# Row transposes of the first four key chunks tied to later projections in a hand-planned attention list

## The chip, the cores and the metric

The kernel runs on one core of a Trainium2 chip. The metric is the device time of one execution in microseconds (us). The core has five engines with in-order queues of their own: TensorE (PE in the profile, with its weight loads as PEld), VectorE (DVE), ScalarE (ACT), GpSimd (POOL) and SyncE (SP), which here issues most of the transfers.

## The reference

One inference step of a two-layer decoder trunk, for a new sequence of 512 tokens (prompt) and for 8 sequences of 4 new tokens each with 256 past tokens in a paged key/value cache (sample). Layer 0 mixes tokens with a gated convolution, layer 1 with stick-breaking attention; each layer ends in a convolutional feed-forward network (FFN). All data are 32-bit floats; the model width is 1024, with 16 heads of 64.

```python
def stick_breaking_block(q, k, v, bias, q_start):
    z = jnp.einsum('bqhd,bkhd->bhqk', q, k) * (HEAD_DIM ** -0.5) + bias
    valid = k_pos < q_pos
    log_fail = jnp.where(valid, jax.nn.log_sigmoid(-z), 0.0)
    after = lax.cumsum(log_fail, axis=3, reverse=True) - log_fail
    weights = jnp.where(valid, jnp.exp(jax.nn.log_sigmoid(z) + after), 0.0)
    return jnp.einsum('bhqk,bkhd->bqhd', weights, v)

# layer 1
qkv = (h @ attn_w_qkv).reshape(b, t, 3, N_HEADS, HEAD_DIM)
q, k, v = qkv[:, :, 0], qkv[:, :, 1], qkv[:, :, 2]
att = stick_breaking_attention(q, concat(k_past, k), concat(v_past, v), bias, past_len)
x = x + att.reshape(b, t, -1) @ attn_w_o
new_k.append(k); new_v.append(v)      # the new K and V rows are outputs too
```

The last line is what the change is about: the new keys, token by token, are an output of the kernel.

## The kernel before, in words

All 544 tokens are worked on together, transposed: a chunk of 128 features lies on the 128 partitions and the tokens along the free dimension. A matrix product is made from 128x128 weight blocks that are split into a high and a low part (`whi` by ACT, line 401, `wlo` by DVE, line 404) and three matmuls for each block (lines 2150 to 2152 in the attention stage). Tokens are taken in two halves, the first with 256 columns and the second with 288.

The stages are layer 0's convolution, its FFN together with the queries and the first four key chunks of layer 1, the attention stage, layer 1's FFN and the final norm. In each stage the code does not issue instructions directly. It fills a list (`Plan`) with operations, each with an engine, an assumed cost and what it reads and writes; `Plan.run` then goes through the list with those assumed costs as a clock and so settles, before the kernel is compiled, in which order each engine gets its work. For an engine that comes free it takes an operation that is ready or soon will be, by the assumed time, with a bonus of 0.04 us for each microsecond of work that hangs on it (`EAGER`). Operations marked as fill are taken when nothing else is ready soon, or when their bonus outweighs the wait. The chip then runs each engine's queue strictly in that order, whatever the real times are.

The attention list is built by the calls at the end of the listing. For each of the 8 chunks of two heads it holds `keys(c, h)` and `values(c, h)` for the two token halves h, `page_logits` for the decode sequences' cached keys, and `pair(c)`, the prompt's attention for the two heads of a chunk:

- `project(slot, h)` (line 2159) adds four fill operations on PE, a quarter each, of six matmuls, into a bank `acc` (two of them). All projections follow one another in the order v0, v1, v2, k4, v3, k5, v4, k6, v5, k7, v6, v7, each with both halves.
- `to_rows` (line 2174) turns two 128x128 blocks into token rows with two PE transposes (line 2180) into the bank `one`, of which there is only one.
- `keys` (line 2185): for c of 4 and up it projects the chunk first. For c below `EARLY_K` = 4 the keys are already there from the stage before. Either way it calls `to_rows`, copies the rows to a buffer `kr` (DVE, line 2195; two buffers) and stores them to the output (SP, line 2196, 128 KB).
- `values` (line 2199): projects, copies to a buffer `vT` (ACT, line 2203; two buffers), calls `to_rows`, and copies the rows to `vtok` (DVE, line 2207), which the products `av` of `pair` read (line 2475).
- `page_logits`: pages of cached keys, gathered by POOL (line 2042) into three buffers, are transposed in halves of four PE transposes (line 2271) into a bank `t` (one of them) and copied from it by DVE or ACT in turn (line 2278). The second half of the very first page goes to a bank `dz` instead. The list allows 3.0 us before the first pages are there.

Banks and buffers with a name are handed out as a ring: the n-th user of the name waits for the user that held the same bank before, in the order in which the code asks for them. Rows of key chunks 0 and 1 are asked for ahead of the first values, rows of chunk 2 and 3 one and two rounds later. The decode sequences' weights use the bank `one` four times, ahead of the rows of k4.

Of the kernel before, what the change touches and what calls it, by code (L numbers as in the profile page):

```python
# [17 lines left out]
P = 128  # L18
# [27 lines left out]
EARLY_K = 4  # L46
# [204 lines left out]
def tile_trunk(  # L251
# [8 lines left out]
    nc = tc.nc  # L260
    dve, act, pool, pe = nc.vector, nc.scalar, nc.gpsimd, nc.tensor
# [210 lines left out]
    def uid(s):  # L472
        _n[0] += 1
        return f"{s}_{_n[0]}"
# [38 lines left out]
    def begin(n, ready, s0, st, xh, xl):  # L513

        pts = [bank("acc", uid("acc")) for _ in range(n)]
        for i, pt in enumerate(pts):
            gemm(pt, st, s0 + i, xh, xl, None, (0, ready))
        return pts
# [193 lines left out]
    for i in range(2):  # L712
        ch0 = (PE_CHUNKS[0] + i * len(PE_CHUNKS) // 2) * P
        for m in range(8):
            nj = min(4, CW - 4 * m)
            pool.dma_start(out=trow[i][m * n_g:(m + 1) * n_g, :nj * 32].rearrange("g (j h) -> g j h", j=nj),
                          in_=conv_w_dw[0, 4 * m:4 * m + nj, ch0:ch0 + n_g * 32].rearrange("j (g h) -> g j h", h=32))
# [4 lines left out]
    plan = Plan(E_CONV, 0.12, CONV_SHIFTS)  # L722
# [14 lines left out]
    def psum(tag):  # L737
        def make():
            if tag == "acc":
                taken.append(tag)  # L740
            return bank(tag, uid(tag))

        return plan.tile(tag, banks[tag], make)
# [27 lines left out]
    def prepare(slot, begin, place):  # L771

        low = []
        raw = slot // 2
        plan.op("act", 0.95, lambda: begin(low), r=[("raw", slot)], w=[*place, ("slot", slot), "prep"])
        plan.op("dve", 1.135, lambda: low[0](), r=[("raw", slot)], w=[("slot", slot), "low"])
        if slot % 2:
            plan.op(f"raw{raw}", 5.4 if raw else 8.6, lambda: None, w=[("raw", slot + 2 * RAW_BUFS + i) for i in (-1, 0)], r=[("slot", slot)])
# [50 lines left out]
    def conv_vector(c, lo, n):  # L829


        acc = buf(conv, "dwh", [P, 256], 1) if n == 256 else buf("ctmp", "dwa", [P, SEQ], 2)
        keys = ext(c) if n > 256 else ext(c, 1, 2, 3) if lo else ext(c, 0, 1)
        done = ext(c) if n > 256 else ext(c, 1, 2, 3) if lo else ext(c, 0)
        halves = [("y", c, h) for h in range(2) if lo <= 256 * h < lo + n]
        cost = n * 1.05e-3 + 0.126
        for k in range(CW):
            src = ext_p[:, c, lo + k:lo + k + n]
            if k == 0:
                plan.op("act", 0.28 + n * 0.85e-3, lambda src=src: act.activation(  # L840
                    acc()[:, :n], src, AF.Identity, scale=pcol(0, c), bias=pcol(R_BDW, c)), r=[*keys, "prm"], w=[acc])
            elif k < CW - 1:
                plan.op("dve", cost, lambda k=k, src=src: dve.scalar_tensor_tensor(
                    acc()[:, :n], src, pcol(k, c), acc()[:, :n], op0=ALU.mult, op1=ALU.add),
                    r=[*keys, "prm"], w=[acc])
            else:
                plan.op("dve", cost, lambda k=k, src=src: dve.scalar_tensor_tensor(
                    yc[:, c, lo:lo + n], src, pcol(k, c), acc()[:, :n], op0=ALU.mult, op1=ALU.add),
                    r=[acc, "prm"], w=halves + done)
# [55 lines left out]
    def add_sum(c, h):  # L905
        c0, n = STREAMS[h]
        if c == 0:
            return
        keys = [("y", i, k) for i in ((0, 1) if c == 1 else (c,)) for k in ((1, 2) if h else (0,))]

        def add():
            o = late["ysum"][:, c0:c0 + n]
            dve.tensor_tensor(o, yc[:, c, c0:c0 + n], yc[:, 0, c0:c0 + n] if c == 1 else o, op=ALU.add)

        plan.op("dve", 0.08 + n * 1.05e-3, add, r=keys, w=[("sum", h)])
# [191 lines left out]
    for c in range(0, NC, 2):  # L1107
# [9 lines left out]
        for cc in range(2):  # L1117
            plan.op("act", 0.33, lambda c=c, cc=cc, pt=pt: act.copy(
                ext_s[:, c + cc, :, 0:PAST], pt()[:, cc * 240:(cc + 1) * 240].rearrange("p (b t) -> p b t", b=NB)),
                r=[pt, "junk"], w=[("past", c + cc)])  # L1120
# [124 lines left out]
    for h, (c0, n) in enumerate(STREAMS):  # L1245
        if h:
            layer_norm(1)
        for g in (0, 4):
            for i in range(4):
                c = g + i  # L1250
# [5 lines left out]
        if not h:  # L1256
# [8 lines left out]
            r=[nrm.acc[0]], w=[ms])  # L1265
    plan.op("act", 0.34, lambda: act.activation(rs()[:, :n], ms()[:, :n], AF.Sqrt, bias=eps_t[:, 0:1], scale=1.0),
            r=[ms, "table"], w=[rs])
    plan.op("dve", 1.7, lambda: dve.reciprocal(rs()[:, :n], rs()[:, :n]), w=[rs])
    for c in range(NC):
# [3 lines left out]
                r=[rs, ("x", c, 0)], w=[u])  # L1273
# [4 lines left out]
            r=[u, ("XH", c, 0)], w=[("XL", c, 0)], lift=NLIFT)  # L1278
# [767 lines left out]
    qT, kT, kT_s, dz = (att[k] for k in ("qT", "kT", "kT_s", "dz"))  # L2046
# [14 lines left out]
    def rows_q(j, bg):  # L2061
        rows = slice(j * HD, (j + 1) * HD)
        return rows, qT[rows, :, SEQ + 16 * bg:SEQ + 16 * bg + 16].rearrange("p c (b i) -> p c b i", b=4)
# [7 lines left out]
    for bg in range(2):  # L2071
        for j in range(2):
            rows, src = rows_q(j, bg)
# [4 lines left out]
    kpv = k_p[0, 0].rearrange("(b p) h d -> p b (h d)", p=P)  # L2078
# [23 lines left out]
    plan = Plan()  # L2102
# [13 lines left out]
    def sbuf(tag, w, bufs, dt=F32, pool_=va):  # L2116
        return plan.tile(tag, bufs, lambda: pool_.tile([P, w], dt, tag=tag, name=uid(tag), bufs=bufs))
# [10 lines left out]
    def acost(n):  # L2128
        return 0.1 + n * 0.95e-3
# [12 lines left out]
    def weighted(pt, slot, h, q):  # L2142

        c0, n = (SA, SB)[h]

        def f():
            hi, lo, _ = W.w[slot]
            o = pt()[:, :n]
            for k in (2 * q, 2 * q + 1):
                pe.matmul(o, hi[:, k, :], XH[:, k, c0:c0 + n], start=(k == 0), stop=False)  # L2150
                pe.matmul(o, hi[:, k, :], XL[:, k, c0:c0 + n], start=False, stop=False)
                pe.matmul(o, lo[:, k, :], XH[:, k, c0:c0 + n], start=False, stop=(k == NC - 1))

        return f
# [4 lines left out]
    def project(slot, h):  # L2159

        n = (SA, SB)[h][1]
        pt = psum("acc")
        last = order[0]
        for q in range(4):

            last = plan.op("pe", 6 * n * COL, weighted(pt, slot, h, q), w=[pt], follows=last, after=[] if last is None else [last],
                           r=[("slot", slot), ("X", 2 * q), ("X", 2 * q + 1)])
            plan.fill.add(last)
        order[0] = last
        if h:  # L2170
            prepare(slot + SPLIT_BUFS)
        return pt

    def to_rows(src, r):

        rows = psum("one")

        def turn():
            for b in range(2):
                pe.transpose(rows()[:, b * P:(b + 1) * P], src(b), ident)  # L2180

        plan.op("pe", 0.22, turn, r=r, w=[rows])
        return rows, (lambda: rows()[:, :2 * P].rearrange("p (b d) -> p b d", b=2))

    def keys(c, h):
        c0, n = (SA, SB)[h]
        if c >= EARLY_K:
            pt = project(k0 + TURNS.index(("k", c)), h)
            plan.op("act", acost(256), lambda: act.copy(kT[:, c, c0:c0 + 256], pt()[:, :256]),
                    r=[pt], w=[("k", c, h)] + ([("ktp", i) for i in range(4)] if c >= 4 else []))  # L2190
            if h:
                plan.op("act", 0.2, lambda: act.copy(kT_s[:, c, :], pt()[:, 256:n]), r=[pt], w=[("kT_s", c)])
        rows, src = to_rows(lambda b: kT[:, c, c0 + b * P:c0 + (b + 1) * P], [("k", c, h)])
        kr = sbuf("kr", 2 * P, 2)
        plan.op("dve", 0.38, lambda: dve.tensor_copy(kr().rearrange("p (b d) -> p b d", b=2), src()), r=[rows], w=[kr])
        plan.op("sp", 3.0, lambda: nc.sync.dma_start(out=kpv[:, 2 * h:2 * h + 2, c * P:(c + 1) * P],
                                                     in_=kr().rearrange("p (b d) -> p b d", b=2)), r=[kr])

    def values(c, h):
        n = (SA, SB)[h][1]  # L2200
        pt = project(k0 + TURNS.index(("v", c)), h)
        vt = plan.tile("vT", 2, lambda: vts_.tile([P, SA[1]], F32, tag="vT", name=uid("vT"), bufs=2))
        plan.op("act", acost(256), lambda: act.copy(vt(), pt()[:, :256]), r=[pt], w=[vt])
        if h:
            plan.op("act", 0.2, lambda: act.copy(vT_s[:, c, :], pt()[:, 256:n]), r=[pt], w=[("vT_s", c)])
        rows, src = to_rows(lambda b: vt()[:, b * P:(b + 1) * P], [vt])
        plan.op("dve", 0.38, lambda: dve.tensor_copy(vtok[c % 3][:, 2 * h:2 * h + 2, :], src()),
            r=[rows], w=[("vtok", c % 3, h)])
        if h:
            plan.op("sp", 3.0, lambda: nc.sync.dma_start(out=vpv[:, :, c * P:(c + 1) * P], in_=vtok[c % 3]),  # L2210
                    r=[("vtok", c % 3, 0), ("vtok", c % 3, 1)])
# [325 lines left out]
    for i, tag in enumerate(("acc", "z", "z", "one")):  # L2537
        pt = psum(tag)
        begun.append(pt)
        last = None  # L2540
        for q in range(4):
            last = plan.op("pe", 6 * SA[1] * COL, weighted(pt, o0 + i, 0, q), w=[pt], follows=last,
                           r=[("slot", o0 + i)] + [("X", k) for k in (2 * q, 2 * q + 1)])
# [3 lines left out]
    for j in range(2):  # L2547
        rows = slice(j * HD, (j + 1) * HD)
# [57 lines left out]
```

## Time and profile before

| what | value |
|---|---|
| median of 3 runs (lowest, highest) | 1285.38 us (1284.53, 1286.04) |
| the profiled execution's own time | 1286.91 us |
| its span, first to last instruction | 1285.2 us |
| mean granted clock of TensorE | 0.993 of full speed |
| transposes of key blocks into bank `one` (line 2180) | 32, median 273 ns, first at 654.2 us, last at 822.0 us |
| copies to `kr` (line 2195) | 16, median 418 ns, first at 657.9 us, last at 822.4 us |
| stores of `kr` (line 2196) | 16, 128 KB each |

The profile lists the instructions of one execution with start and duration in us from the first instruction. "Idle before" is how long the engine stood still ahead of an instruction, and the arrow names what released it. Matmuls overlap, so that the busy time of PE counts some of it twice and the start of one to the start of the next is the time that it really takes. The granted clock of TensorE is given as a share of full speed.

### The profile page before, as it was taken

How to read it: one execution, taken by the hardware profiler on the slowest of the kernel's cores; microseconds unless marked ns; L12 is line 12 of the kernel's file. 1: busy time of each engine (PE TensorE's matmuls, PEld its weight loads, DVE VectorE, ACT ScalarE, POOL GpSimd, SP SyncE). 2: the span in 40 equal slices, each digit the busy share in tenths (PEclk: the TensorE clock that was granted, in tenths of full speed). 3: DMA queues.
4: the chain of work that ended last, by engine and by line, in shares of the span. 5: the costliest groups of instructions: out<-in, count | busy, mean ns of one | idle time of the engine just before them, and what ended most of it. 6: DMA issues, size and time to landing. Idle time of an engine off the chain costs nothing. (4 is left out here: it accounts for less than half of the span.)

```text
span 1285.2 us, 26447 instructions
## 1 busy us (share of the span) xinstructions
PE 1262.4 (98%) x10822; PEld 1208.1 (94%) x10822; DVE 1014.1 (79%) x1712; ACT 720.3 (56%) x1440; POOL 165.6 (13%) x291
## 2 busy tenths in 40 slices
PE   9999999999999999999979899999999999999998
PEld 8997699999999999999967788899999999999998
DVE  7999877978977877779847489766988986886863
ACT  7794584645654545545546488754645555454453
POOL 5000014101001000002113235100111011000000
PEclk9999999999999999999989999999999999999999
DMA  8365423223233232244355536233132333233221
GB/s 224 125 177 145 111 72 109 66 67 99 91 117 94 88 117 91 83 145 157 99 164 152 169 107 193 83 116 99 51 100 84 99 117 110 72 103 97 91 76 71
DMA packets 119180, 142.39 MB, mean 111 GB/s; under 512 B 5102, under 2 KB 110246, under 8 KB 118787
## 3 DMA queue, kind: packets, MB, share of 16 engines
q1 hardware_dynamic: 110350, 111.89, 28.0%
q0 software_dynamic: 8704, 28.80, 7.1%
q8 instruction: 85, 1.39, 0.4%
q14 instruction: 37, 0.30, 0.1%
q10 hardware_dynamic: 4, 0.01, 0.0%
HBM read 129.34 MB, written 12.18 MB: 110 GB/s over the span
## 5 line engine op out<-in xcount | busy, mean ns | idle before, releaser
L401 ACT CAST whi<-raw 128x1024 fp32r<-128x1024 f32 (+2 forms) x249 | 225.4, 909 | 125.8 <-PE av L1406 24.3
L404 DVE TENSOR_TENSOR wlo<-raw,whi 128x1024 fp32r<-128x1024 f32 (+2 forms) x249 | 260.2, 1048 | 31.6 <-ACT whi L401 30.2
L759 PE MATMUL acc<-XH,whi 128*128 128x288 f32 (+1 forms) x384 | 112.9, 294 | 0.0
L761 PE MATMUL acc<-XH,wlo 128*128 128x288 f32 (+1 forms) x384 | 110.5, 288 | 0.9 <-DVE wlo L404 0.9
L760 PE MATMUL acc<-XL,whi 128*128 128x288 f32 (+1 forms) x384 | 110.5, 288 | 0.0
L1405 PE MATMUL av<-HH,whi 128*128 128x288 f32 (+1 forms) x280 | 83.4, 298 | 0.4 <-DVE xT L1720 0.4
L1631 PE MATMUL acc<-TH,wlo 128*128 128x272 f32 x288 | 83.1, 289 | 0.0
L1630 PE MATMUL acc<-TL,whi 128*128 128x272 f32 x288 | 82.9, 288 | 0.0
L1629 PE MATMUL acc<-TH,whi 128*128 128x272 f32 x288 | 82.9, 288 | 0.0
L1406 PE MATMUL av<-HL,whi 128*128 128x288 f32 (+1 forms) x280 | 82.8, 296 | 0.0
L1407 PE MATMUL av<-HH,wlo 128*128 128x288 f32 (+1 forms) x280 | 82.5, 295 | 0.0
L1665 ACT COPY G<-acc 128x272 f32<-128x272 f32 (+1 forms) x72 | 26.7, 371 | 95.0 <-PE acc L1631 95.0
L1405 PE MATMUL tr<-HH,whi 128*128 128x256 f32 (+1 forms) x280 | 79.3, 283 | 0.0
L1406 PE MATMUL tr<-HL,whi 128*128 128x256 f32 (+1 forms) x280 | 79.1, 282 | 0.0
L1407 PE MATMUL tr<-HH,wlo 128*128 128x256 f32 (+1 forms) x280 | 78.6, 281 | 0.0
L759 PEld LDWEIGHTS acc<-XH,whi 128*128 128x128 f32 x384 | 72.3, 188 | 1.4 <-issue 0.4
L761 PEld LDWEIGHTS acc<-XH,wlo 128*128 128x128 f32 x384 | 72.3, 188 | 1.1 <-DVE wlo L404 1.1
L760 PEld LDWEIGHTS acc<-XL,whi 128*128 128x128 f32 x384 | 72.3, 188 | 0.3
L1568 DVE SCALAR_TENSOR_TENSOR cv<-G,fprm,cv 128x560 f32<-128x560 f32 x88 | 69.5, 797 | 0.5
L1631 PE MATMUL acc<-XH,wlo 128*128 128x272 f32 x240 | 69.4, 289 | 0.0
L1630 PE MATMUL acc<-XL,whi 128*128 128x272 f32 x240 | 69.2, 288 | 0.0
L1629 PE MATMUL acc<-XH,whi 128*128 128x272 f32 x240 | 69.0, 287 | 0.0
(477 smaller groups left out, 4412.4 us busy)
## 6 DMA issues: line engine op xcount, KB each, us to landing
raw<-in_ffn_w_gate_dram SPq DMA_DIRECT2D x22, 1024.0 KB
raw<-in_ffn_w_up_dram SPq DMA_DIRECT2D x22, 1024.0 KB
raw<-in_ffn_w_down_dram SPq DMA_DIRECT2D x24, 768.0 KB
raw<-in_attn_w_qkv_dram SPq DMA_DIRECT2D x12, 1024.0 KB
raw<-in_conv_w_in_dram POOLq DMA_DIRECT2D x6, 1024.0 KB, 7.1
rep<-glu SPq DMA_DIRECT2D x36, 142.0 KB
raw<-in_conv_w_out_dram POOLq DMA_DIRECT2D x4, 1024.0 KB, 5.9
raw<-in_ffn_w_down_dram SPq DMA_DIRECT2D x8, 512.0 KB
```

The lines of the kernel that those rows point to most:

```text
L401: act.copy(hi[:, k, :], src[:, k])
L404: dve.tensor_tensor(lo[:, k, :], src[:, k], hi[:, k, :], op=ALU.subtract)
L759: pe.matmul(o, hi[:, k, :], XH[:, k, c0:c0 + n], start=(k == 0), stop=False)
L760: pe.matmul(o, hi[:, k, :], XL[:, k, c0:c0 + n], start=False, stop=False)
L761: pe.matmul(o, lo[:, k, :], XH[:, k, c0:c0 + n], start=False, stop=(k == NC - 1))
L1405: pe.matmul(o, hi[:, j + k, :], xh, start=(start and k == 0), stop=False, **kw)
L1406: pe.matmul(o, hi[:, j + k, :], xl, start=False, stop=False, **kw)
L1407: pe.matmul(o, lo[:, j + k, :], xh, start=False, stop=(stop and k == len(xs) - 1), **kw)
L1568: plan.op("dve", 0.73, lambda k=k: dve.scalar_tensor_tensor(s(), g()[:, k:k + M], fcol(3 * l + k, f), s(), op0=ALU.mult, op1=ALU.add), r=[ ...
L1629: pe.matmul(o, hi[:, j + k, :], xh, start=(start and k == 0), stop=False, **kw)
L1630: pe.matmul(o, hi[:, j + k, :], xl, start=False, stop=False, **kw)
L1631: pe.matmul(o, lo[:, j + k, :], xh, start=False, stop=(k == 3), **kw)
```

## The change

Rows of key chunks 0 to 3 are no longer put into the list where `keys` is called. `keys` puts a function for them at the end of a queue, `early`. Each time `project` has added the second half of a projection, it takes the oldest function from that queue and lets it add its operations there, with the projection's last quarter as a dependency of the transposes. So the rows of chunk 0's two halves hang on v0 and v1, those of chunk 1 on v2 and k4, those of chunk 2 on v3 and k5 and those of chunk 3 on v4 and k6. Key chunks 4 to 7 are handled as before. The operations themselves (two transposes, a copy, a store) are the same.

```diff
@@ project(slot, h)
         order[0] = last
         if h:
             prepare(slot + SPLIT_BUFS)
+            if early:
+                early.popleft()([last])
         return pt
 
-    def to_rows(src, r):
+    early = deque()
+
+    def to_rows(src, r, after=()):
...
-        plan.op("pe", 0.22, turn, r=r, w=[rows])
+        plan.op("pe", 0.22, turn, r=r, w=[rows], after=after)
...
@@ keys(c, h)
-        rows, src = to_rows(lambda b: kT[:, c, c0 + b * P:c0 + (b + 1) * P], [("k", c, h)])
-        kr = sbuf("kr", 2 * P, 2)
-        plan.op("dve", 0.38, lambda: dve.tensor_copy(kr().rearrange("p (b d) -> p b d", b=2), src()), r=[rows], w=[kr])
-        plan.op("sp", 3.0, lambda: nc.sync.dma_start(out=kpv[:, 2 * h:2 * h + 2, c * P:(c + 1) * P],
-                                                     in_=kr().rearrange("p (b d) -> p b d", b=2)), r=[kr])
+
+        def out(after=()):
+            rows, src = to_rows(lambda b: kT[:, c, c0 + b * P:c0 + (b + 1) * P], [("k", c, h)], after)
+            kr = sbuf("kr", 2 * P, 2)
+            plan.op("dve", 0.38, lambda: dve.tensor_copy(kr().rearrange("p (b d) -> p b d", b=2), src()), r=[rows], w=[kr])
+            plan.op("sp", 3.0, lambda: nc.sync.dma_start(out=kpv[:, 2 * h:2 * h + 2, c * P:(c + 1) * P],
+                                                         in_=kr().rearrange("p (b d) -> p b d", b=2)), r=[kr])
+
+        early.append(out) if c < EARLY_K else out()
```

## The prediction

> **What bounds the kernel now.** I read the page first, then busy time by stretch, then the waits, then the instructions one by one where the waits sit.
>
> ```profile
> span 1285.2 us, 26447 instructions
> PE 1262.4 (98%) x10822; PEld 1208.1 (94%) x10822; DVE 1014.1 (79%) x1712; ACT 720.3 (56%) x1440; POOL 165.6 (13%) x291
> ```
>
> TensorE (PE) is busy for 98% of the span, so only time in which PE stands still, or runs slowly, can be won. The attention list, which the change edits, runs from 654 to 862 us. The columns below are the stretch, its length, then busy time and instructions of PE, its weight load, DVE, ACT and POOL, the granted clock, and DMA.
>
> ```profile
> 654.24:672.29 18.05, 11.81 (x66) 9.56 (x64) 7.08 (x11) 6.23 (x9) 3.12 (x4) 0.72 0.47 147
> 672.29:742.00 69.71, 65.02 (x566) 53.11 (x566) 43.08 (x63) 37.71 (x65) 20.37 (x24) 0.98 0.51 155
> 742.00:862.00 120.00, 118.11 (x1289) 104.30 (x1287) 94.07 (x145) 92.78 (x169) 33.01 (x38) 1.00 0.42 134
> ```
>
> The first 18 us are the weak place: PE is idle for 6.2 us of them and its clock averages 0.72. From 742 on it has next to no gap, so what is saved at the start reaches the end unless something later runs dry. Two rows of the waits name the cause:
>
> ```profile
> PE one L2180 <- DVE kr L2195: 6.2, 2, 3.5
> DVE kr L2195 <- DMA out_dram<-kr: 4.2, 1, 4.2
> ```
>
> The row transposes of the first key chunks wait twice for the copy of the rows before them (6.2 us), and one such copy waits 4.2 us for a store. The instructions show how (start, duration, engine, line; idle time before it in brackets):
>
> ```profile
> 654.24 0.38 PE L2180 MATMUL one<-ident,kT 128*128 128x128 f32 x2
> 654.55 1.13 PE L2413 MATMUL z<-kT,qT 64*128 64x512 f32 x4
> 655.60 2.36 DVE L404 TENSOR_TENSOR wlo<-raw,whi 128x1024 fp32r<-128x1024 f32 x2 [0.72 <-ACT whi L401]
> 657.88 0.42 DVE L2195 COPY kr<-one 128x256 f32<-128x256 f32 x1
> 658.35 0.44 PE L2180 MATMUL one<-ident,kT 128*128 128x128 f32 x2 [2.67 <-DVE kr L2195]
> 658.41 7.76 SPq L2196 DMA_DIRECT2D out_dram<-kr  x4
> 658.62 0.60 PE L2271 MATMUL t<-ident,xT 128*128 128x128 f32 x4
> 659.06 0.76 PE L2271 MATMUL dz<-ident,xT 128*128 128x128 f32 x4
> 659.26 0.69 DVE L2278 COPY kT<-t 128x512 f32<-128x512 f32 x1
> 660.04 1.08 PE L2271 MATMUL t<-ident,xT 128*128 128x128 f32 x4
> 660.10 0.98 POOL L2042 DMA_INDIRECT xT<-in_cache_k_dram,idx  x1 [22.98 <-PE dz L2271]
> 664.14 0.42 DVE L2195 COPY kr<-one 128x256 f32<-128x256 f32 x1 [4.19 <-DMA out_dram<-kr]
> 664.62 0.69 PE L2180 MATMUL one<-ident,kT 128*128 128x128 f32 x2 [3.50 <-DVE kr L2195]
> 665.22 1.12 PE L2271 MATMUL t<-ident,xT 128*128 128x128 f32 x4
> 667.41 1.06 PE L2271 MATMUL t<-ident,xT 128*128 128x128 f32 x4
> 669.55 0.63 PE L2271 MATMUL t<-ident,xT 128*128 128x128 f32 x4
> 670.85 0.66 PE L2271 MATMUL t<-ident,xT 128*128 128x128 f32 x4
> 672.29 0.66 PE L2271 MATMUL t<-ident,xT 128*128 128x128 f32 x4
> ```
>
> All engines run their queues in order. The first key copy stands on DVE behind two weight splits that end at 657.96; the second transposes need the single bank `one` back and hold PE until 658.35. The third copy needs a `kr` buffer whose store was issued at 658.41 and holds DVE until 664.14. Behind it on DVE is the copy of a page half (L2278), so the page transposes on PE, eight halves from 658.62 to 672.29, stop too.
>
> **What the change does to this start.** The four chunk 0 and 1 transposes leave it. They now wait for the last quarters of projections v0, v1, v2 and k4, those of chunks 2 and 3 for v3, k5, v4 and k6: one pair at a time, so that a store has long landed when its buffer is wanted again. With them gone the list's only ready PE work at its start is the four z matmuls, fill (projection quarters of six matmuls) and, after the 3.0 us that the list allows for the first pages, the page halves. By the list's costs I expect the z matmuls, one fill quarter, halves 1 and 2, half 3, and from there one quarter between each two halves. A quarter takes 0.70 us:
>
> ```profile
> 685.49 0.28 PE L2150 MATMUL acc<-XH,whi 128*128 128x256 f32 x1
> 686.19 0.38 PE L2180 MATMUL one<-ident,vT 128*128 128x128 f32 x2
> ```
>
> The clock of the new start: z from 654.24 to 655.37 (1.13 long), the quarter to 656.07, halves 1 and 2 at 0.44 each (658.62 to 659.06) to 656.95. Half 3 needs bank `t`, which DVE empties only after the splits: 657.96 + 0.69 = 658.65. So the first wait doesn't vanish, it goes to the splits: PE idles about 1.75 us where it idled 2.67. Half 3 starts at 658.70, and with undisturbed steps of 1.44 (670.85 to 672.29) half 8 starts at 658.70 + 5 x 1.44 = 665.90. Before it was 672.29: 6.39 us earlier.
>
> To that comes fill: six quarters are done by then (one, and five between halves 3 and 8), before it was four (one between each two of halves 4 to 8): 2 x 0.70 = 1.40 us more. Against it, the four transposed pairs are still to be made, 0.31 each (654.24 to 654.55): 1.24 us. Chunks 2 and 3 owe the same PE work at either place, 0. Sum so far: 6.39 + 1.40 - 1.24 = 6.55 us.
>
> **The clock.** It fell after the long idle time and made two of the eight steps 2.19 (665.22 to 667.41) and 2.14 us (667.41 to 669.55) long instead of 1.44.
>
> ```profile
> 658.00:660.00 2.00, 1.65 (x12) 1.50 (x12) 1.41 (x3) 0.14 (x1) 0.00 (x0) 0.84 0.36 62
> 660.00:662.00 2.00, 1.12 (x6) 0.71 (x4) 0.00 (x0) 0.44 (x1) 0.98 (x1) 0.50 0.99 335
> 668.00:670.00 2.00, 2.00 (x14) 2.00 (x12) 0.69 (x1) 0.00 (x0) 0.00 (x0) 0.60 0.75 250
> 734.00:736.00 2.00, 2.00 (x13) 2.00 (x13) 1.93 (x4) 0.50 (x2) 0.51 (x1) 0.61 0.08 25
> 733.61 0.39 PE L2150 MATMUL acc<-XH,whi 128*128 128x256 f32 x1 [1.75 <-ACT kT L2189]
> ```
>
> The clock is at 0.84 in the 2 us after the 2.67 us gap and at 0.61 after one of 1.75 (733.61). Such a gap of 1.75 is what stays, so a fall costs up to 2.19 + 2.14 - 2 x 1.44 = 1.45 us; a start that keeps its clock costs 0. The second row is the nearer one, but smaller gaps stood before it, so I take half, 0.70.
>
> The Trainium skill ("TensorE: Matmul & The Clock Gate", Part 1, "What's actually happening") has the clock halved after an idle window of about 3.4 us and given back after a busy one. By that a gap of 1.75 leaves it whole; the sum would then be without this term. The trace differs on the first half, as the gap of 2.67 shows, and agrees on the second as far as it can be seen: the clock is back by 670 after PE resumes at 664.62.
>
> **What is late next.** Five of the moved pairs (the last of chunk 1 and all of chunks 2 and 3) now come where bank `one`, handed out in the order in which the code asks for it, is dense:
>
> ```profile
> 765.88 0.40 DVE L2195 COPY kr<-one 128x256 f32<-128x256 f32 x1
> 792.04 0.42 DVE L2207 COPY vtok<-one 128x256 f32<-128x256 f32 x1
> 793.84 0.42 DVE L2195 COPY kr<-one 128x256 f32<-128x256 f32 x1
> 797.71 0.42 DVE L2195 COPY kr<-one 128x256 f32<-128x256 f32 x1
> 769.88 0.44 PE L2180 MATMUL one<-ident,vT 128*128 128x128 f32 x2
> 770.56 0.36 ACT L2203 COPY vT<-acc 128x256 f32<-128x256 f32 x1
> 771.24 0.29 PE L2150 MATMUL acc<-XH,whi 128*128 128x288 f32 x1
> ```
>
> Ten uses of the bank (k4, v3, k5, v4, k6, two each) lie from 765.88 to 797.71, 31.8 us; back to back a use takes 1.8 (792.04 to 793.84). Fifteen need 27 us and fit. But v4's first half leaves its accumulator only at 770.56, right after v3's first rows (769.88) free a `vT` buffer, while fill goes on at 771.24: the two are in balance. After the change these rows are one use (1.8 us) later, and fill is 1.40 + 0.31 = 1.7 us ahead, so up to 3.5 us pass with no fill. PE has other work there; the cost is 0 to 3.5 and I take a third, 1.20, since PE was busy for 118.11 of 120.00 us on other work and fill together.
>
> Edits at nothing: eight DVE copies of 0.42 move to a DVE busy for 94 of 120 us, hidden by PE; uncovered they are 3.4 us. On SP eight stores pass behind weight loads that are asked for well ahead; if a load were held up by a `kr` wait it would cost the 1.8 us of one use. On POOL the first gather follows half 2 and so goes from 660.10 to about 657; it must land before half 7, at 664.46.
>
> ```profile
> DMA to landing us min/median/max: 4.0/4.7/6.9
> ```
>
> Even the slowest, 6.9, lands at 663.9. The sum: 6.55 - 0.70 - 1.20 = 4.65 us. The profiled execution took 1286.9 with a span of 1285.2, the median is 1285.38; I take the difference off the median: **1280.7 us**.
>
> **The rivals.**
> 1. *The clock holds, by the rule above:* 6.55 - 1.20 = 5.35, so 1280.0. For it: the gap shrinks by a third. Against: the row at 733.61.
> 2. *Nothing dries up later either, or the denser start fills more gaps:* 6.55 gives 1278.8. At most all that the first stretch lost can come back. Its useful work is z 1.13, four pairs 1.24, seven halves 3.08 and four quarters 2.80, 8.25 of 18.05 us, so 9.8 at the outside: 1275.6.
> 3. *The gain is given back:* the list picks anew after every small change. If fill is held for all of 3.5 us and a gap like that at 733.61 with its slow clock (1.75 + 1.45) opens once, 6.55 - 0.70 - 3.5 - 3.2 = -0.85, about 1286.2: no change. Against: PE has hardly a gap after 742.
> 4. *Slower: bank `one` becomes the chain.* If the five added uses can't be overlapped, all later rows, and with them the last values and the end, come 5 x 1.8 = 9.0 us later; with the 3.5 of fill and the 1.45 of clock the balance is 6.55 - 9.0 - 3.5 - 1.45 = -7.4, so 1292.8; from 4 uses unhidden with half of the rest it is slower by 3.1 (6.55 - 7.2 - 2.5). It decides once the free bank time, 31.8 - 18 = 13.8, falls under 9. Against: that room.
>
> That the transposes stay where they were can't be: each waits for a projection's last quarter.
>
> **How the numbers follow.** A measurement tells about 0.2% (2.6 us) from no change. Forecast 0.32 and rival 1 0.20, both inside 1278.5 to 1282.5; rival 2 0.15; rival 3 0.19; rival 4 0.14. Faster 0.67, same 0.19, slower 0.14. The range goes from between rival 2's two ends, 1276, to 1289, which leaves out the worst of rival 4 and the last of rival 2.
>
> **What would show it.** Right: no wait of `one` on `kr` in the list's first 20 us, one fill quarter ahead of the first page half, a wait of about 1.75 us on DVE's page copy, half 8 near 666, no `kr` copy waiting for a store, and a list that ends some 4 to 6 us earlier. Wrong: half 8 near 666 but PE gaps after 740, above all fill (L2150) waiting for ACT's `vT` copy, or rows through `one` that av products wait for.

## The result and the profile after

The changed kernel takes 1280.29 us (median of 5 runs, 1279.19 to 1282.87) beside 1285.70 us for the kernel before in the same job (5 runs, 1284.53 to 1287.89): a ratio of 0.9958 [0.9943, 0.9973]. Measured once more on another occasion (`r_after`, below) it took 1282.05 us beside 1285.68, 0.9968 [0.9959, 0.9977]. Over all 16 runs of it the median is 1281.94, over the 74 runs of before in all jobs 1285.70: 3.8 us faster. The profiled execution took 1282.87 us, the slowest of its five.

The page of the kernel after, first its span and busy times:

```profile
span 1281.2 us, 26454 instructions
PE 1261.4 (98%) x10822; PEld 1205.3 (94%) x10822; DVE 1015.3 (79%) x1712; ACT 720.6 (56%) x1440; POOL 163.1 (13%) x291
```

The busy times are those of before, the span is 4.0 us shorter. The same three stretches of the attention list, counted from its start at 655.16 (columns as before):

```profile
655.16:673.21 18.05, 16.21 (x135) 12.13 (x135) 11.20 (x14) 11.10 (x16) 6.71 (x8) 1.00 0.53 175
673.21:742.92 69.71, 64.48 (x546) 53.09 (x546) 42.52 (x62) 38.30 (x70) 18.66 (x22) 0.98 0.43 138
742.92:858.21 115.29, 112.38 (x1240) 98.49 (x1238) 90.95 (x142) 86.78 (x157) 28.73 (x37) 1.00 0.45 145
```

In its first 18.05 us PE now executes 135 instructions where it executed 66, at a clock of 1.00 instead of 0.72. The list is 858.21 - 655.16 = 203.05 us long, before 862.22 - 654.24 = 207.98 (the ends are the first matmul of the stage that follows, before and then after in the rows below). That is 4.93 us less. The list began 0.92 us later in this run, by work ahead of it that is the same; in all the profiles of this study its start lies between 654.24 and 656.44 us. What follows the list takes 423.0 us in both.

```profile
862.22 0.37 PE L498 MATMUL acc<-XH,whi 128*128 128x288 f32 x1 [1.27 <-ACT sq L569]
858.21 0.40 PE L498 MATMUL acc<-XH,whi 128*128 128x288 f32 x1 [0.52 <-DVE xT L2567]
```

The start, instruction by instruction:

```profile
655.16 1.13 PE L2421 MATMUL z<-kT,qT 64*128 64x512 f32 x4
655.80 2.36 DVE L404 TENSOR_TENSOR wlo<-raw,whi 128x1024 fp32r<-128x1024 f32 x2
656.22 0.39 PE L2150 MATMUL acc<-XH,whi 128*128 128x256 f32 x1
657.04 0.60 PE L2279 MATMUL t<-ident,xT 128*128 128x128 f32 x4
658.08 0.69 DVE L2286 COPY kT<-t 128x512 f32<-128x512 f32 x1
658.35 0.98 POOL L2042 DMA_INDIRECT xT<-in_cache_k_dram,idx  x1 [20.41 <-PE dz L2279]
658.83 0.66 PE L2279 MATMUL t<-ident,xT 128*128 128x128 f32 x4 [0.75 <-DVE kT L2286]
663.53 0.38 PE L2184 MATMUL one<-ident,vT 128*128 128x128 f32 x2
664.83 0.63 PE L2279 MATMUL t<-ident,xT 128*128 128x128 f32 x4 [0.92 <-DMA xT<-in_cache_k_dram,idx]
666.24 0.66 PE L2279 MATMUL t<-ident,xT 128*128 128x128 f32 x4
```

The z matmuls, one fill quarter (656.22), page halves 1 and 2 (657.04 for the first), half 3 after a short wait for DVE's page copy (658.83), and then half after half with fill between them. The last row is half 8, 666.24 - 655.16 = 11.08 us after the list's start, where it was 672.29 - 654.24 = 18.05. No row transposes of keys are left here; the first copy to `kr` comes at 676.9 us. Half 7 (664.83) waits 0.92 us for the gather that POOL issued at 658.35.

PE's waits in the list of the kernel after, without two of 0.7 us that the next rows show (waiting for what: us in all, times, longest):

```profile
PE dz L2359 <- DMA xT<-in_cache_v_dram,idx: 1.8, 1, 1.8
PE t L2279 <- DVE e L2286: 1.6, 2, 0.8
PE acc L2150 <- ACT kT L2193: 1.6, 1, 1.6
PE t L2279 <- DVE kT L2286: 1.0, 2, 0.8
PE t L2279 <- DMA xT<-in_cache_k_dram,idx: 0.9, 1, 0.9
PE one L2184 <- DVE kr L2201: 0.5, 1, 0.5
```

The 6.2 us of `one` behind `kr` are down to 0.5, and no copy to `kr` waits for a store any more. The first row, 1.8 us for a gather of cached values, belongs to this run: the second profile of the same kernel doesn't have it, and there the list takes 857.28 - 655.78 = 201.50 us. The third row is fill that waits for ACT, in a place that the prediction did not name:

```profile
718.15 0.66 PE L2279 MATMUL t<-ident,xT 128*128 128x128 f32 x4 [0.78 <-DVE e L2286]
719.53 0.66 PE L2279 MATMUL t<-ident,xT 128*128 128x128 f32 x4 [0.73 <-ACT e L2286]
720.98 0.66 PE L2279 MATMUL t<-ident,xT 128*128 128x128 f32 x4 [0.78 <-DVE e L2286]
722.36 0.81 PE L2463 MATMUL t<-ident,e 128*128 128x128 f32 x4 [0.73 <-ACT e L2286]
728.24 0.64 ACT L2193 COPY kT<-acc 128x256 f32<-128x256 f32 x2
728.65 0.39 PE L2150 MATMUL acc<-XH,whi 128*128 128x256 f32 x1 [1.56 <-ACT kT L2193]
724.00:726.00 2.00, 2.00 (x24) 0.94 (x20) 0.00 (x0) 0.38 (x1) 0.00 (x0) 0.50 1.03 396
```

Fill is used up here. Both `acc` banks hold k4, whose copy to `kT` (728.24) has to wait until the last page logits have been made: key chunks 4 to 7 take the place in which the turned pages lie. With no fill the page halves follow one another with gaps of 0.73 to 0.78 us, as each waits for the copy of the one before, and the clock falls to 0.50 (last row, same columns as the stretches). Before, fill reached further: two such gaps (rows below) and then the 1.75 us at 733.61, 3.26 in all. Now it is 0.78 + 0.73 + 0.78 + 0.73 + 1.56 = 4.58.

```profile
727.37 0.66 PE L2271 MATMUL t<-ident,xT 128*128 128x128 f32 x4 [0.78 <-DVE e L2278]
728.75 0.66 PE L2455 MATMUL t<-ident,e 128*128 128x128 f32 x4 [0.73 <-ACT e L2278]
```

### The profile page after: what moved, and what is told of

Same layout as the page of the kernel before. It is cut to its first block, busy times and chain, and to the rows that moved or that the text cites. A ratio compares the mean times of both kernels' runs of the same rounds, so it can differ in the third digit from the quotient of the medians.

```text
span 1281.2 us, 26454 instructions
## 1 busy us (share of the span) xinstructions
PE 1261.4 (98%) x10822; PEld 1205.3 (94%) x10822; DVE 1015.3 (79%) x1712; ACT 720.6 (56%) x1440; POOL 163.1 (13%) x291
```

## The experiments

The theory at the outset: the gain is the wait of one DVE copy for a store, nothing else, and the idle time and slow clock that follow from it. Against it stood that the new place of the transposes or the new order pays, or the release one by one, or that the slow steps at the start have a cause of their own.

**Only the store wait (`e1_kr4`).** The kernel before, with two more buffers. The queues of all engines keep the order of before, instruction for instruction.

```diff
-        kr = sbuf("kr", 2 * P, 2)
+        kr = sbuf("kr", 2 * P, 4)
```

> The kernel before with four kr buffers instead of two; every engine's queue keeps its order, only the third and fourth key copies no longer wait for a store. Theory A (the loss is the two waits of the transposes, the larger of them the store's, and the slow clock after them): the 3.5 us wait goes, the first one of 2.67 stays, half 4 comes some 4 us earlier, and the median falls by 3.5 to 5 us, most of what the change won. Rival B (the gain comes from the new order of the whole list, fill moved ahead): little, under 1.5 us, is won here, since no order changes. Rival C (the slow clock after the first gap of 2.67 us is the loss): half 4 comes earlier but the steps stay at 2.1 us, and 1.5 to 3 us are won.

Measured: 1282.04 us (6 runs, 1280.70 to 1284.67) beside 1286.07, 0.9967 [0.9955, 0.9979], 4.0 us faster. PE's instructions at the start:

```profile
660.37 0.44 PE L2180 MATMUL one<-ident,kT 128*128 128x128 f32 x2 [2.49 <-DVE kr L2195]
663.54 0.64 PE L2180 MATMUL one<-ident,kT 128*128 128x128 f32 x2
664.53 0.66 PE L2271 MATMUL t<-ident,xT 128*128 128x128 f32 x4 [0.36 <-DVE kT L2278]
670.08 0.66 PE L2271 MATMUL t<-ident,xT 128*128 128x128 f32 x4
```

The list starts at 656.44 here. The first wait, behind the weight splits, is still 2.49 us; the second, 3.50 before, is gone (663.54). Half 8 (670.08) comes 13.64 us after the start instead of 18.05, 4.41 earlier, and the list is 203.59 us long, 4.39 less: what is won at the start arrives at the end in full. So two more buffers alone bring as much as the whole change did. The long steps, 2.19 and 2.14 us before, are gone with the wait, so they have no cause of their own.

**Release of all waiting rows at once (`e2_all`).** The changed kernel; every second half of a projection empties the queue, so the chunks go in as they come.

```diff
-            if early:
+            while early:
                 early.popleft()([last])
```

> The changed kernel, but each end of a second projection half releases all rows that are waiting, not one pair: chunks 0 and 1 hang together on v0, chunk 2 on v1, chunk 3 on v2. Theory A: the start is as in the changed kernel and so is the time, within 1.5 us, as rows released in a bunch stand among other ready work. Rival D (one by one is what counts): the kr store makes DVE and PE wait again in the middle of the list, by 2 to 4 us, and half or more of the gain is gone.

Measured: 1281.21 us (6 runs, 1279.79 to 1283.64), 0.9968 [0.9956, 0.9980]. Within the noise this is the changed kernel's time: that rows are released one by one is worth nothing that can be measured.

**Only chunks 0 and 1 (`e3_two`).** The changed kernel; chunks 2 and 3 are handled as before.

```diff
-        early.append(out) if c < EARLY_K else out()
+        early.append(out) if c < 2 else out()
```

> The changed kernel, but only the rows of chunks 0 and 1 go through the queue; chunks 2 and 3 stand where they stood before the change. Theory A, with my charge of 1.2 us for the dense stretch of bank one: five added uses there become none or one, and the time is 0 to 1.2 us below the changed kernel's. Rival (rows of chunks 2 and 3 earn something by going late): 1 us or more above it.

Measured: 1281.41 us (5 runs, 1279.15 to 1283.19), 0.9961 [0.9947, 0.9974]. The same again. That four fewer pairs pass through bank `one` in its dense part doesn't show.

**No rows of chunks 0 to 3 at all (`e4_none`).** This kernel leaves out those eight pairs of transposes, their copies and their stores, and with them that part of the new keys; its time is a rough floor for what another placing of them could reach, rough because the planner picks the order anew here too.

```diff
-        early.append(out) if c < EARLY_K else out()
+        None if c < EARLY_K else out()
```

> The changed kernel with the rows of key chunks 0 to 3 left out altogether (eight pairs of transposes, their copies and stores; those key outputs are not written). Theory A: PE is the bound where they now stand, so 8 x 0.31 = 2.5 us less than the changed kernel, 2 to 4 with the eased bank. Rival (they are hidden where they now stand): the same time within 1 us.

Measured: 1279.37 us (5 runs, 1278.82 to 1281.63), 0.9954 [0.9941, 0.9968]: 0.9 us below the changed kernel's first measurement and 2.6 below the median of its 16 runs. Eight pairs at 0.31 us are 2.5 us of PE; between that and nothing this experiment does not decide. By this floor better placing alone could bring no more than about 2.6 us.

**The changed kernel again (`r_after`)**, to have its median from more runs and a second profile.

> The changed kernel once more, beside the three below. All theories: 0.9958 of before, within 0.0015. Its second trace tells which of the gaps of the first (1.84 us for a page of values, the clock) belong to the kernel and which to the run.

Measured: 1282.05 us (11 runs, 1279.59 to 1283.68). Half 8 comes 667.13 - 655.78 = 11.35 us after the list's start, half 3 after a wait of 1.13 us, half 7 after 0.81 us for its gather: the first profile's start, within 0.4 us.

**The clock alone (`e5_warm`).** This is the kernel before, but PE makes 24 and 32 transposes more into a bank that nobody needs yet, ahead of the two pairs of row transposes that wait. The planned order is that of before.

```diff
         def turn():
+            for b in range(idle):
+                pe.transpose(spare()[:, b % 4 * P:(b % 4 + 1) * P], src(b % 2), ident)
             for b in range(2):
...
+                            {(0, 1): 24, (1, 1): 32}.get((c, h), 0))
```

> The kernel before, with 24 more transposes ahead of the second pair of row transposes and 32 ahead of the fourth (results unused, into the bank of pair 0's products), so that PE works through the two waits and does not idle; nothing else moves. Theory A with a clock term: the granted clock stays near 1.0, the steps of 2.19 and 2.14 us shrink to about 1.4, and the median falls by 1.2 to 2.3 us, though both waits stay. Rival (the clock costs nothing, because the page halves are paced by the copies out of bank t): within 0.7 us of before.

Measured: 1284.91 us (11 runs, 1283.77 to 1286.39) beside 1285.68, 0.9992 [0.9983, 1.0001], 0.8 us. The two stretches of 8 us at the start, first of before, then of this kernel:

```profile
654.00:662.00 8.00, 4.46 (x26) 2.90 (x24) 4.25 (x6) 3.86 (x4) 0.98 (x1) 0.84 0.34 99
662.00:670.00 8.00, 5.38 (x27) 5.07 (x27) 2.14 (x4) 0.58 (x1) 0.95 (x1) 0.52 0.67 225
```

```profile
654.00:662.00 8.00, 7.87 (x64) 6.71 (x63) 5.04 (x7) 4.47 (x6) 0.67 (x1) 1.00 0.22 57
662.00:670.00 8.00, 7.70 (x64) 6.85 (x63) 2.07 (x4) 0.91 (x2) 1.34 (x3) 1.00 0.75 250
```

The clock holds at 1.00 instead of 0.84 and 0.52, while the waits stay (DVE's for the store is 3.8 us; the added transposes only fill them). By the medians the fall of the clock at the start thus costs 0.8 us (between 0 and 2.2 by the interval) of the 4.0, less than the 1.2 to 2.3 expected: the bigger part is the standing still itself.

**The order alone, by the planner's bonus (`e6_up`, `e7_down`).** The kernel before, with the bonus of the attention list at 0.042 and at 0.038 instead of 0.04. Nothing else is changed; both waits at the start stay (2.50 and 3.89 us in the first of the two, 2.01 and 2.65 in the second).

```diff
-    plan = Plan()
+    plan = Plan(eager=0.042)
```

> The kernel before with a bonus of 0.042 in place of 0.04 in the attention list alone: the start keeps its order with both waits, the later list is picked anew. Theory A: within 2 us of before, as the loss at the start stays. Rival E (a new order of the list is worth as much as the change): 3 us or more off, either way.

> The kernel before with a bonus of 0.038 in place of 0.04 in the attention list: the start as before, the later list picked anew. With the run at 0.042 (1.8 us above before) it gives the size of what a new order alone does. Theory A: within 2.5 us of before. Rival E: 3 us or more off.

Measured: 1287.50 us (11 runs), 1.0017 [1.0008, 1.0026], and 1288.74 us (9 runs), 1.0023 [1.0013, 1.0033]: 1.8 and 3.1 us slower. The second is over the 2.5 us that the theory allowed to chance, and in the range of its rival E (3 us or more). In `e6_up` PE's order is that of before up to 833 us; the same 261 matmuls from there to the list's end then take 30.68 us instead of 29.11, so in these traces the loss lies there. An order picked anew can thus be worth nearly as much as the measured gain. The change picks anew too, so its 3.8 us are the store wait plus or minus something of this kind, and only `e1_kr4`, which keeps the order, isolates the former.

**A version that fills the gap at 718 (`e8_swap`).** The changed kernel, but v3 is projected ahead of k4, and asked for ahead of the decode weights, so that an `acc` bank comes free while the pages are still being turned.

```diff
-    TURNS = [("v", 0)] + [x for c in range(NC) for x in (("k", c + 2), ("v", c + 1))
+    TURNS = [("v", 0)] + [x for c in range(NC) for x in ((("k", c + 2), ("v", c + 1)) if c != 2 else (("v", c + 1), ("k", c + 2)))
...
         if c == 2:
+            both_halves(values, c + 1)
             decode_weights()
...
-        if c + 1 < NC:
+        if c + 1 < NC and c != 2:
```

> The changed kernel, with the third values chunk projected ahead of key chunk 4 and asked for ahead of the decode weights. Key chunk 4 cannot leave its accumulators until the last page logits are done, since its place holds cached keys; fill stands still there and PE idles for 4 to 5 us in pieces of 0.7 to 1.6 around 718 to 728. Theory F (that idle time is the largest one left): v3's eight quarters fill it, and the time is 2 to 4 us below the changed kernel's. Rival: the wait comes later by as much, or bank one gets no denser and no easier, and the time is within 1.5 us.

Measured: 1275.13 us (5 runs, 1275.07 to 1277.85) beside 1285.68, 0.9924 [0.9911, 0.9938]. That is the best of the study, 10.5 us below before and 6.8 below the 16 runs of the changed kernel, where 2 to 4 were expected. The stretch from 715 to 740, first in the changed kernel and then here:

```profile
715.00:740.00 25.00, 20.41 (x156) 15.39 (x155) 14.36 (x22) 14.13 (x26) 4.41 (x6) 0.93 0.34 120
```

```profile
715.00:740.00 25.00, 23.70 (x192) 20.06 (x192) 15.79 (x25) 15.52 (x29) 5.97 (x8) 1.00 0.53 170
818.45:850.45 32.00, 32.00 (x303) 30.45 (x303) 21.97 (x42) 21.64 (x47) 3.21 (x4) 1.00 0.38 125
850.45 0.36 PE L498 MATMUL acc<-XH,whi 128*128 128x288 f32 x1
```

PE is busy for 3.3 us more of the 25, at a full clock. But the list's last 32 us are full as well (second row), where the changed kernel has 31.39 and before 29.95, and the stage after the list starts with no wait at all (third row; 0.52 and 1.27 us in the other two). So two things changed, and the next three runs tell them apart.

**The same swap elsewhere (`e9_swap_before`, `e10_swap_kr4`, `e12_swap_two`).** On the kernel before; on before with four `kr` buffers (the same order of the queues as the first); and on the changed kernel with only chunks 0 and 1 queued, as in `e3_two`.

> The kernel before (key rows released together, two kr buffers) with only the swap of v3 and key chunk 4. Theory A: the start's loss and the loss around 718 to 728 are separate, so the swap is worth here what it was worth on the changed kernel, 5 to 7 us, and the change is worth 4 to 5 on top: 1279 to 1281. Rival G (the two gains overlap, since each only gives fill to the same empty places): 1276 to 1277.5.

> The kernel before with the swap and with four kr buffers, rows still released together. Theory A (the store's wait is most of what the change wins): 1275.5 to 1277.5, within 2 us of the changed kernel with the swap. Rival B (moving the transposes is what counts): 3 us or more above it.

> The changed kernel with the swap and only chunks 0 and 1 in the queue. Theory A with a dense bank one: 0 to 1 us below the changed kernel with the swap (1275.1), since v3 has left the dense stretch already. Rival: 1 us or more above.

Measured, beside 1285.68:

| kernel | median, runs | ratio |
|---|---|---|
| `e9_swap_before` | 1288.45 us (11) | 1.0018 [1.0009, 1.0027] |
| `e10_swap_kr4` | 1284.10 us (11) | 0.9984 [0.9975, 0.9994] |
| `e12_swap_two` | 1285.93 us (11) | 1.0003 [0.9994, 1.0012] |

None of them comes near `e8_swap`, and theory A missed all three. `e10_swap_kr4` and `e12_swap_two` came out where their rivals put them, 9.0 and 10.8 us above `e8_swap`. So with the swap the store wait, worth 4.35 us here (below), is not most of the 13.3 us between `e9_swap_before` and `e8_swap`; but to move only the rows that waited, as `e12_swap_two` does, doesn't bring the rest. The stretch from 715 to 740 is not the reason: it is as full as there in the first (25.00) and in the third (23.70). The last 32 us of the list and the first matmul behind it are, in `e9_swap_before` and then in `e12_swap_two`:

```profile
830.00:862.00 32.00, 25.57 (x238) 23.16 (x237) 14.34 (x30) 14.31 (x31) 0.95 (x2) 0.96 0.34 116
861.58 0.58 PE L498 MATMUL acc<-XH,whi 128*128 128x288 f32 x1 [3.98 <-ACT sq L569]
```

```profile
828.00:860.00 32.00, 26.39 (x247) 23.99 (x246) 14.63 (x29) 13.60 (x32) 0.40 (x2) 1.00 0.37 124
859.77 0.37 PE L498 MATMUL acc<-XH,whi 128*128 128x288 f32 x1 [3.16 <-DVE xT L2568]
```

Here the list runs dry at its end: PE stands still for 6.4 and 5.6 of 32 us, 3.98 and 3.16 of them right ahead of the next stage's first matmul. What follows the list takes 425.1 and 424.5 us here, where it takes 423.0 in before and after. The filled middle is paid back there. Against `e9_swap_before`, `e10_swap_kr4` differs in nothing but the two buffers, and it is 4.35 us faster: the store wait has about the same price on a second order.

## Why the prediction came true, step by step

The time forecast was 1280.7 us; it came out at 1280.3 and 1282.05. The likeliest case was right in what pays. Its terms were right in the first, and less so in the others. That the sum came so close is in part luck: a clock fall that was charged (0.70) didn't come, a quarter of fill that was counted (0.70) is missing, and the charge of 1.20 for one place matches what was lost at another. The runs had their luck too: the first five had a mean clock of 0.998 or 0.999, while eight of the later eleven had 0.996 or 0.997.

- **The wait for the store is the gain: shown.** `e1_kr4` takes only this wait away, with every queue in the same order, and gains 4.0 us; `e10_swap_kr4` against `e9_swap_before` gains 4.35. Rival 3, in which the gain is lost on the way, did not occur, though its reason ("the list picks anew") is real: a slightly different bonus alone costs 1.8 and 3.1 us.
- **The start: 6.39 us predicted for half 8, 6.97 and 6.70 measured.** The order was z, one quarter, halves 1 and 2, half 3, as predicted. The remaining first wait was put at 1.75 us and is 0.75 and 1.13; in these two runs the list starts at 655.16 and 655.78, later against the weight splits than in the trace of before. In `e2_all`, whose list starts at 654.59, it is 1.65. Fill was put at six quarters; it was five: half 7 waited for its gather, and v0's first rows (663.53) took the place of the sixth.
- **"Even the slowest, 6.9, lands at 663.9" failed.** Counted from the list's start, that was 663.9 - 654.24 = 9.66 us, for a half 7 wanted at 10.22. In the trace half 7 starts at 9.67, but PE was free for it 0.92 us sooner, at 8.75, since half 3 came 0.79 us sooner than forecast and the quarter ahead of half 7 is missing. The landing was sized rightly; that the need for it moves forward with everything else was not.
- **The clock at the start: 0.70 charged, nothing measured.** After gaps of 0.75 and 1.13 us (1.65 in `e2_all`) it stays at 1.00 through the whole first stretch. For the start, rival 1 was right. The Trainium skill ("TensorE: Matmul & The Clock Gate", Part 1, "What's actually happening") has the clock halved after an idle window of about 3.4 us. That these shorter gaps left it whole agrees with that. The row at 733.61 was no sure sign of a fall: `e5_warm` and `e2_all` have the same wait of 1.75 us, and their clock stays at 1.00 behind it. By `e5_warm` the whole fall in the kernel before is worth 0.8 us in the medians, with an interval that doesn't exclude the upper bound of 1.45; in the two traces half 8 comes 16.01 us after the start with the clock held and 18.05 without, 2.04 more. The trace that the prediction was read from is not the usual case, either: its mean clock is 0.993, as in 7 of the 69 runs of before that were taken beside the experiments, and these average 1287.1 us. The 53 at 0.996 and 0.997 average 1285.6.
- **What is late next: 1.20 charged for v4 at `vT` and bank `one`; the place was wrong.** Bank `one` holds PE for 0.46 us once, `e3_two` with four fewer pairs in it has the same time, and rival 4 falls. The give-back is at k4 instead: fill that runs further ahead fills both `acc` banks earlier, and k4 can't be copied out until the pages are done. There idle time grows from 3.26 to 4.58, by 1.32 us, and the clock falls earlier. That this is close to the 1.20 charged is chance. The row at 733.61, quoted in the prediction for the clock only, was this very wait; its meaning for fill was overlooked. With it rival 2, in which nothing dries up, falls too.
- **What the sum did not have.** The last 32 us of the list are fuller by 31.39 - 29.95 = 1.44 us in the first profile. Relative to the start the second profile's list is 6.48 us shorter: 6.70 for half 8, 0.70 for a fifth quarter, 0.31 for v0's rows, less 1.24 for the four pairs, 1.17 at k4 (4.43 of idle time there), and 1.41 at its end (31.36 of the last 32) give 6.71. In the medians only 3.6 to 5.4 arrive: the second profile's list starts 1.54 us later than that of before, and the profiled execution of before is one of the slower ones. The list starts up to 2.2 us apart in runs of the same work, which is far more than the difference between the change (3.8) and `e1_kr4` (4.0), so whether the new order adds anything to the store wait stays open.

Also open is why the order of `e8_swap` has fill left for its last 32 us and that of `e12_swap_two` has not. The traces agree with fill spent early being missed late, but no run changed that alone.

## What to carry to other kernels

Where an in-order queue stands behind a buffer, look up what the buffer waits for: here two more output buffers did what the whole rearrangement did, and kept the order. Test a change to a planned list beside a twin that keeps the order of every queue, and beside one that changes only the order: here order alone moved the time by 1.8 to 6.8 us. And filling a gap in the middle paid only in the one order that had fill left for its end, so read the last stretch of the list first.

## What was unexpected of the hardware

The clock falls after less idle time than one would think from the single gaps, and not each time. In the kernel after the 2 us windows from 722 on show 0.68 and 0.50 behind a row of gaps of 0.78, 0.73, 0.78 and 0.73 us within 5 us; a gap of 0.75 and one of 0.92 with full work between them, at the start, leave it at 1.00. In shorter windows there the clock is 1.00 or 0.50 (1.00 from 722.50 to 722.70, 0.50 from 722.75 to 723.00), so 0.68 means that it fell within the 2 us. In the second profile the same row of gaps comes 0.9 us later, and so does the fall, within 0.2 us:

```profile
722.00:724.00 2.00, 1.64 (x16) 0.86 (x20) 0.00 (x0) 1.10 (x3) 0.85 (x1) 0.68 1.10 401
```

```profile
722.00:724.00 2.00, 1.27 (x12) 0.86 (x16) 0.00 (x0) 0.62 (x2) 0.95 (x1) 0.95 1.04 359
724.00:726.00 2.00, 2.00 (x21) 0.85 (x23) 0.00 (x0) 1.14 (x2) 0.00 (x0) 0.50 1.07 402
```

No idle time here reaches the window of about 3.4 us after which the Trainium skill ("TensorE: Matmul & The Clock Gate", Part 1, "What's actually happening") has the clock halved, so here row and rule differ, as they did for the 2.67 us gap of before. The gaps alone don't settle it, though. In `e2_all` PE stands still for 1.27, 0.78, 0.73 and 1.75 us between 719.78 and 728.74, and the clock stays at 1.00, as the last gap and the windows around it show:

```profile
728.74 0.39 PE L2150 MATMUL acc<-XH,whi 128*128 128x256 f32 x1 [1.75 <-ACT kT L2193]
726.00:728.00 2.00, 0.99 (x12) 0.42 (x4) 1.38 (x4) 1.41 (x3) 0.00 (x0) 1.00 1.01 361
728.00:730.00 2.00, 1.26 (x10) 1.26 (x11) 1.97 (x3) 1.45 (x4) 1.15 (x2) 1.00 0.30 118
```

What decides between the two stays open.

The time of one kernel goes with its mean granted clock: of the 16 runs of the changed kernel the five at 0.996 have a mean of 1282.6 us, the three at 0.999 one of 1280.0.
